# Front of a hybrid decoder block: the row scale of the activations moved to Pool, the first pieces reordered, two streams joined

## The chip, the cores and the metric

The kernel runs on one core of one Trainium2 chip. A core has TensorE (PE: matmul; PEld: its weight loads), VectorE (DVE), ScalarE (ACT), GpSimd (POOL) and SyncE (SP, which here only issues DMAs). The metric is the device time of one execution in microseconds (us).

## The reference

One layer of a decoder block over 256 tokens and 1024 channels, all in float32. `h = rms_norm(x, attn_norm_w)` is projected by one wide matrix `w_in`; slices of the result feed three token mixers: a retention, a gated short convolution and NSA attention (16 heads, 4 key groups). Each mixer's output is projected and gated, the sum goes through an output projection onto `x`, then a convolutional GLU feed-forward block and a last norm follow.

```python
h = rms_norm(x, attn_norm_w)                 # x * rsqrt(mean(x*x) + eps) * w
z = h @ w_in
rq, rk, rv, rg, sb, sc, sx, nq, nkv, ng, mg = split(z)
kc = gelu(blocks(k_c + pos) @ cmp_w1[0]) @ cmp_w2[0]     # compressed keys; vc likewise with index 1
o  = g0 * attend(nq, kc, vc) + g1 * attend_selected(nq, k_s, v_s) + g2 * attend_window(nq, k_w, v_w)
y_sc = sb * causal_dwconv(sc * sx, sc_conv_w)
merged = sigmoid(mg) gates * (y_ret @ w_ret_out, y_sc @ w_sc_out, o @ w_nsa_out)
```

With 4 blocks of 64 tokens and 16 to be selected, every block is selected.

## The kernel before

**Numbers.** Every float32 operand of a matmul is cut into a high and a low part of type fp32r, and a product is three matmuls (`mm3`: high by high, high by low, low by high).

**Pieces.** The weights come in pieces of 1 MB, each two halves of 128x1024 elements. A piece is an `Item`: `load` issues its two DMAs on SP's queue into the ring `raw` of 4 buffers; `split` makes the parts, a cast on ACT (line 131, `whi`) and a subtraction on DVE (line 132, `wlo`), which also frees the raw buffer; `consume` runs the matmuls. Parts lie in a ring of 5 pairs, to which the front adds one more (`w_m`). `stream` walks over a list of items: it loads two ahead, splits one ahead, consumes, and then runs what earlier items put off with `later`. With a generator `gen` it pulls that many steps of the attention after an item as the item's `pull` says.

**Order on the engines.** Within an engine instructions start in queue order. The queues are laid out when the kernel is built, by a planner that has the written order as its priority; so instructions of neighbouring items are interleaved on DVE and ACT, and one that waits holds up those behind it.

**Kinds of piece.** `f_consume` makes 48 matmuls of 128x256 into one PSUM buffer of the ring `mm` (3 buffers), which its `evac` empties. `t_pair` makes two pieces of 24 matmuls of 128x512 each; its first piece takes two buffers of `mm` for both pieces, and the evacuations come with the second. A `w1` piece has 16 matmuls of 128x256 into a buffer of the ring `aux`.

**The front.** The items are, in this order: five pieces `vv` (values and attention gates, on the unscaled `xw`), `kc` and `vc` (also on `xw`; their evacuation multiplies by the row scale `rstd`, line 329, shifts a copy by DMA and makes the blocks `bb` later, lines 346 and 347), `ks` and `kw` (on `hT`, the normed activations), then `g_sc[0]` (a gate of the `mg` columns), `w1` 0, `nq` 0 (queries), `g_sc[1]`, `w1` 1, `g_sc[2]`, `w1` 2, `g_sc[3]`, `w1` 3. `w1` 0 and 1 are the compressed keys' branch and read `bb` of `kc`; `w1` 2 and 3 are the values' and read `bb` of `vc`. The buffers of `mm` go round: `kc`, `vc`, `ks`, `kw` take numbers 0, 1, 2, 0; `g_sc[0]` takes 1 and 2; `nq` 0 takes 0 again.

`head_h` makes `hT` in two halves, ahead of the matmuls of `kc` and of `vc`: for each of 8 blocks of 128 channels DVE multiplies `xT_s` in place by the norm weight `attw(k)` and `rstd` (line 299); for each pair ACT casts to `hTh` (line 302) and DVE subtracts for `hTl` (line 303). `rstd` lies in 128 partitions; it comes from a sum of squares that POOL adds up (lines 270 and 272).

`key_evac` empties `ks` and `kw`: four casts on ACT (line 361, `kdh`) and four subtractions on DVE (line 362, `kdl`) in turn, and four copies to the other half of the partitions, issued on POOL's queue (line 365).

**The attention stream.** After the front its temporary tiles are given back, and a second call of `stream` runs 23 items (`q1 x0 x1 ... n3`: queries, short convolution, its projection, gates) and pulls 36 steps of the attention between them.

Of the kernel before, what the change touches and what calls it, by code (L numbers as in the profile page):

```python
# [13 lines left out]
AF = mybir.ActivationFunctionType  # L14
OP = mybir.AluOpType
# [3 lines left out]
S = 256  # L19
# [44 lines left out]
def kernel(  # L64
# [15 lines left out]
    V, A, T, G = nc.vector, nc.scalar, nc.tensor, nc.gpsimd  # L80

    def f32(ap):
        return ap.bitcast(F32)
# [9 lines left out]
    def bank(tag):  # L93
        t = psum.tile([128, 512], F32, tag=tag, name=f"ps_{tag}", bufs=3 if tag == "mm" else 5)
        return t
# [39 lines left out]
    def halves(name, i):  # L135
        w = wp[_INDEX[(name, i)]]
        return [(w[:, 0:1024], 1024), (w[:, 1024:2048], 1024)]
# [14 lines left out]
    def piece(name, i, consume, **kw):  # L152
        return Item(halves(name, i), consume, **kw)
# [4 lines left out]
    def mm3(o, l, r, start, stop):  # L158
        (lh, ll), (rh, rl) = l, r
        mm(o, lh, rh, start, False)  # L160
        mm(o, lh, rl, False, False)
        mm(o, ll, rh, False, stop)
# [4 lines left out]

        pending.append(f)

    def stream(items, gen=None, la=2, ls=1):  # L170
        n = len(items)
        for i in range(-la, n):
            if 0 <= i + la < n and not items[i + la].raw:
                items[i + la].load()
            if 0 <= i + ls < n and not items[i + ls].parts:
                items[i + ls].split()
            if i < 0:
                continue
            due = pending[:]
            pending.clear()  # L180
            items[i].consume(items[i].parts)
            for f in due:
                f()
            for _ in range(items[i].pull):
                if gen is not None:
                    next(gen, None)

    def f_consume(act, evac, kmajor=False):


        def go(parts):
            ah, al = act() if callable(act) else act
            ps = bank("mm")
            order = [(b, k) for k in range(KB) for b in range(2)] if kmajor else [(b, k) for b in range(2) for k in range(KB)]
            for n, (b, k) in enumerate(order):
                hi, lo = parts[b]
                c = slice(k * 128, (k + 1) * 128)
                o = ps[:, b * 256 : (b + 1) * 256]
                start = n == 0 if kmajor else k == 0
                mm3(o, (hi[:, c], lo[:, c]), (ah[:, k, :], al[:, k, :]), start, k == KB - 1)  # L200
            evac(ps)

        return go
# [28 lines left out]
    hT = [yp.tile([128, KB, S], F32R, tag=n, name=n) for n in ("hTh", "hTl")]  # L232
    M = []
    rstd = yp.tile([128, S], F32, name="rstd")
# [4 lines left out]
    xT_s = x_s[:, HD:].rearrange("p (k t) -> p k t", k=KB)  # L239
# [14 lines left out]
    def attw(k):  # L254
        return attn_w[:, k : k + 1]
# [39 lines left out]
        spread(rs0, sq[:, 1, :], rstd)  # L295

    def head_h(half):
        for k in range(4 * half, 4 * half + 4):
            V.scalar_tensor_tensor(xT_s[:, k, :], xT_s[:, k, :], attw(k), rstd, op0=OP.mult, op1=OP.mult)  # L299
            if k % 2 == 1:  # L300
                c = slice(k - 1, k + 1)
                A.copy(hT[0][:, c, :], xT_s[:, c, :])
                V.tensor_sub(hT[1][:, c, :], xT_s[:, c, :], f32(hT[0][:, c, :]))  # L303


    att_es = ExitStack()
# [43 lines left out]
    def key_evac(name):  # L350
        def evac(ps):
            p4 = ps.rearrange("p (b t) -> p b t", b=2)
            for par in range(2):
                r = slice(par * 64, par * 64 + 64)
                o = slice(64 - par * 64, 128 - par * 64)
                kv4 = [k.rearrange("p (b two) t -> p b two t", two=2) for k in kd]
                for t in range(2):
                    c = KCOL[(name, t)]
                    src = p4[r, :, t * 128 : (t + 1) * 128]
                    dst = [k[r, :, par, c : c + 128] for k in kv4]  # L360
                    A.copy(dst[0], src)
                    V.tensor_sub(dst[1], src, f32(dst[0]))  # L362
                c = min(KCOL[(name, t)] for t in range(2))
                for k in kv4:
                    nc.gpsimd.dma_start(k[o, :, par, c : c + 256], k[r, :, par, c : c + 256])

        return evac
# [3 lines left out]
    def w1_consume(kv, half):  # L371
        def go(parts):
            if half == 0:
                hid[kv] = bank("aux")
            ps = hid[kv][:, 0:256]
            for q, (hi, lo) in enumerate(parts):
                for l in range(4):
                    lp = half * 8 + q * 4 + l
                    c = slice(l * 256, (l + 1) * 256)
                    mm(ps, blk[kv][:, lp, :], hi[:, c], lp == 0, False)  # L380
                    mm(ps, blk[kv][:, lp, :], lo[:, c], False, lp == 15)
            if half == 1:
                compress_act(kv, ps)

        return go
# [253 lines left out]
    def attention():  # L639
        units = []  # L640
        for g in range(4):
            for par in range(2):
                units.append({"g": g, "par": par, "P": {}})
        cur = {}
        for i in range(len(units) + 1):
            u = units[i] if i < len(units) else None
            v = units[i - 1] if i else None
            if u is not None:
                if u["par"] == 0:
                    cur["pc"] = aw.tile([128, 2, 128], F32, tag="pc", name="pc", bufs=2)  # L650
                    V.memset(cur["pc"], 0.0)
                    cur["y"] = aw.tile([128, 2, S], F32, tag="y", name="y", bufs=2)
                u["y"] = cur["y"]
                u["pc"] = cur["pc"]
            for k in range(4):
                if u is not None:
                    soft_step(u, k // 2, k % 2)
                if v is not None:
                    if k < 3:
                        pt_step(v, k)  # L660
                    if k == 0:
                        v["pcT"] = aw.tile([128, S], F32R, tag="ch", name="ch", bufs=2)
                        pc_step(v)
                    if k:
                        av_step(v, k - 1)
                    if k == 3:
                        out_step(v)
                yield
# [38 lines left out]
    def nqp(g, **kw):  # L707
        return piece("nq", g, f_consume(hT, q_evac(g)), **kw)
# [47 lines left out]
    def gate(n, **kw):  # L756

        return [p for c in range(2) for p in t_pair("mg", GATE[n] * 4 + 2 * c, hT, mg_evac(n, c), **kw)]

    def proj(n, **kw):  # L760
        return [p for c in range(2) for p in t_pair(n, 2 * c, lambda: YY[n], o_evac(n, c), **kw)]
# [3 lines left out]
    items = vv + [  # L765
        then(piece("kc", 0, f_consume(xw, cmp_raw_evac(0))), lambda: head_h(0), before=True),
        then(piece("vc", 0, f_consume(xw, cmp_raw_evac(1))), lambda: head_h(1), before=True),
        piece("ks", 0, f_consume(hT, key_evac("ks"))),
        piece("kw", 0, f_consume(hT, key_evac("kw"))),
        g_sc[0],  # L770
        piece("w1", 0, w1_consume(0, 0)),
        nqp(0),
        g_sc[1],
        piece("w1", 1, w1_consume(0, 1)),
        g_sc[2],
        piece("w1", 2, w1_consume(1, 0)),
        g_sc[3],
        piece("w1", 3, w1_consume(1, 1)),
    ]
    then(vv[3], head_rest)  # L780
# [16 lines left out]
    for c in range(4):  # L797
        if c > 1:
            head_chunk(2 * c, 2 * c + 2)
        head_square(c)  # L800
    V.tensor_scalar(rethalf, x_s[:, KB : 2 * KB], 0.5, None, op0=OP.mult)
    stream(items)
    ysc = [yp.tile([128, KB, S], F32R, tag=n, name=n) for n in ("ysch", "yscl")]
    YY.update(o_sc=ysc)
    splitters.pop()
    cp_es.close()
    aw = aw_es.enter_context(pool("aw"))

    att = attention()
    items = []  # L810
    plan = "q1 x0 x1 x4 b0 x2 x3 q2 x6 b1 x5 x7 b2 q3 b3 s0 s1 n0 n1 s2 s3 n2 n3".split()
    p_sc, g_nsa = proj("o_sc"), gate("o_nsa")
    made = {"x": scx, "b": sbp, "q": nqp, "s": lambda j: p_sc[j], "n": lambda j: g_nsa[j]}
    for n, e in enumerate(plan):
        items.append(made[e[0]](int(e[1])))
        items[-1].pull = (36 * (n + 1)) // len(plan) - 36 * n // len(plan)
    stream(items, att)
    for _ in att:
        pass
    assert not pending  # L820
# [121 lines left out]
    items = [piece("r" + n, i, f_consume(hT, rope_evac(n, i))) for n in "qk" for i in range(2)]  # L942
# [20 lines left out]
    x2, hn, ffb = [], [], []  # L963
# [56 lines left out]
    items = []  # L1020
# [117 lines left out]
    for j in range(NF):  # L1138
        act = x2w if j < NX else lambda: h2
        it = piece("up", j, up_early(j) if j < 2 else f_consume(act, up_evac(j)))  # L1140
# [120 lines left out]
```

## Time and profile before

| | |
|---|---|
| Time, median of 3 runs | 633.57 us (632.41 to 634.73) |
| The profiled execution | 633.64 us, of which the profile's span is 631.9 us |
| Busy: PE | 611.0 us (97%) |
| Busy: DVE | 477.9 us (76%) |
| Busy: ACT | 387.9 us (61%) |
| Busy: POOL | 21.2 us (3%) |
| Moved by DMA | 111.80 MB, mean 177 GB/s |

Times in rows count from the start of the span. The profile gives, for an instruction, its start, its duration, and the idle time of its engine just before it with what ended that wait (the last of several). Matmuls are pipelined, so that one's duration is longer than the distance to the next.

### The profile page before, as it was taken

What the parts mean: (1) busy time and instruction counts of PE and PEld (TensorE: products, weight loads), DVE (VectorE), ACT (ScalarE), POOL (GpSimd) and SP (SyncE); (2) the same over time, 40 slices, a digit from 0 to 9 for tenths busy, and PEclk for the clock granted to TensorE, in tenths of its full rate; (3) what the DMA queues carried; (4) which work ended last, traced back from release to release, by engine and by line L of the source; (5) the groups of instructions that cost most, each with busy time, mean ns of one, the idle gap of its engine ahead of it and who ended that gap; (6) DMA issues with size and microseconds to landing.
All of it is one profiled execution on the core that took longest, in us unless ns stands there. A gap on an engine that the chain in (4) does not pass through costs nothing.

```text
span 631.9 us, 10611 instructions
## 1 busy us (share of the span) xinstructions
PE 611.0 (97%) x3948; PEld 554.9 (88%) x3948; DVE 477.9 (76%) x935; ACT 387.9 (61%) x752; POOL 21.2 (3%) x32
## 2 busy tenths in 40 slices
PE   8986999999999999999999999999999999999994
PEld 7986989999999888899888888888999999999993
DVE  5897667898988877679657976568798777777754
ACT  6665666788888887644545565446756555554532
POOL 4202000000000000000000000000000000000001
PEclk8999999999999999999999999999999999999997
DMA  7759876444354344465664477575347655566401
GB/s 247 239 160 271 243 248 206 135 166 135 104 163 135 108 153 140 134 213 169 203 198 160 133 242 260 192 269 172 108 152 264 213 183 175 183 198 199 136 1 66
DMA packets 32995, 111.80 MB, mean 177 GB/s; under 512 B 3632, under 2 KB 5552, under 8 KB 32816
## 3 DMA queue, kind: packets, MB, share of 16 engines
q1 hardware_dynamic: 30240, 106.00, 51.8%
q10 hardware_dynamic: 1552, 4.08, 2.0%
q0 software_dynamic: 1152, 1.05, 1.1%
q8 instruction: 31, 0.51, 0.3%
q14 instruction: 20, 0.16, 0.1%
HBM read 108.50 MB, written 1.05 MB: 173 GB/s over the span
## 4 chain that ended last, share of the span: by engine, by line
PE 82%; DVE 6%; ACT 5%; DMA 4%; POOL 1%; issue 1%; SPq 0%; POOLq 0%; ACTq 0%
PE ps_mm L156 61%; PE ps_aux L156 18%; DMA raw<-in_wp_dram 3%; DVE wlo L132 2%; ACT whi L131 2%; PE ps_aux L589 1%; DMA xT_s<-in_xT_dram 1%; ACT P L566 1%; POOL sq L272 0%; PE ps_aux L618 0%; DVE hTl L303 0%; DVE dd L329 0%; DVE xT_s L299 0%; ACT low L632 0%; DVE bb L347 0%
## 5 line engine op out<-in xcount | busy, mean ns | idle before, releaser
L132 DVE TENSOR_TENSOR wlo<-raw,whi 128x1024 fp32r<-128x1024 f32 (+1 forms) x197 | 237.7, 1210 | 90.7 <-ACT whi L131 88.7
L131 ACT CAST whi<-raw 128x1024 fp32r<-128x1024 f32 (+1 forms) x197 | 203.2, 1035 | 140.0 <-PE ps_mm L156 98.0
L156 PE MATMUL ps_mm<-hTh,whi 128*128 128x256 f32 x352 | 101.0, 287 | 6.1 <-DVE kdl L362 5.1
L156 PE MATMUL ps_mm<-h,whi 128*128 128x256 f32 x576 | 104.0, 283 | 0.0
L156 PE MATMUL ps_mm<-hTl,whi 128*128 128x256 f32 x352 | 100.4, 285 | 0.6 <-DVE hTl L303 0.6
L156 PE MATMUL ps_mm<-hTh,wlo 128*128 128x256 f32 x352 | 100.5, 285 | 0.3 <-DVE wlo L132 0.2
L156 PEld LDWEIGHTS ps_mm<-h,whi 128*128 128x128 f32 x576 | 90.4, 192 | 0.7
L156 PE MATMUL ps_mm<-h,wlo 128*128 128x256 f32 x288 | 81.5, 283 | 0.0
L156 PEld LDWEIGHTS ps_mm<-hTh,whi 128*128 128x128 f32 x352 | 68.1, 193 | 6.7 <-issue 5.2
L156 PEld LDWEIGHTS ps_mm<-hTl,whi 128*128 128x128 f32 x352 | 68.1, 193 | 1.3 <-DVE hTl L303 1.0
L156 PEld LDWEIGHTS ps_mm<-hTh,wlo 128*128 128x128 f32 x352 | 68.1, 194 | 0.7 <-DVE wlo L132 0.7
L156 PE MATMUL ps_mm<-whi,hTh 128*128 128x512 f32 x152 | 59.7, 393 | 0.0
L156 PE MATMUL ps_mm<-wlo,hTh 128*128 128x512 f32 x152 | 59.3, 390 | 0.0
L156 PE MATMUL ps_mm<-whi,hTl 128*128 128x512 f32 x152 | 59.3, 390 | 0.0
L156 PEld LDWEIGHTS ps_mm<-h,wlo 128*128 128x128 f32 x288 | 55.3, 192 | 0.0
L566 ACT ACTIVATE P<-P,st 128x16 f32<-128x16 f32 (+2 forms) x96 | 37.9, 397 | 0.7 <-DVE st L561 0.7
L156 PE MATMUL ps_aux<-wlo,acth 128*128 128x512 f32 x88 | 34.4, 390 | 0.0
L156 PE MATMUL ps_aux<-whi,acth 128*128 128x512 f32 x88 | 34.4, 390 | 0.0
L156 PE MATMUL ps_aux<-whi,actl 128*128 128x512 f32 x88 | 34.3, 389 | 0.0
L156 PEld LDWEIGHTS ps_mm<-whi,hTl 128*128 128x128 f32 x152 | 28.5, 188 | 6.1
L156 PEld LDWEIGHTS ps_mm<-whi,hTh 128*128 128x128 f32 x152 | 28.6, 188 | 5.6
L156 PEld LDWEIGHTS ps_mm<-wlo,hTh 128*128 128x128 f32 x152 | 28.6, 188 | 5.6
(250 smaller groups left out, 1140.9 us busy)
## 6 DMA issues: line engine op xcount, KB each, us to landing
raw<-in_wp_dram SPq DMA_DIRECT2D x194, 512.0 KB, 4.4
raw<-in_wv_dram SPq DMA_DIRECT2D x8, 280.0 KB, 4.8
x2b<-in_xt_dram ACTq DMA_DIRECT2D x1, 1024.0 KB, 7.2
xT_s<-in_xT_dram SPq DMA_DIRECT2D x3, 256.0 KB, 6.9
rct<-in_rc_dram ACTq DMA_DIRECT2D x1, 768.0 KB, 6.1
kdh<-kdh POOLq DMA_DIRECT2D x4, 128.0 KB, 6.1
kdl<-kdl POOLq DMA_DIRECT2D x4, 128.0 KB, 6.9
finb<-in_fin_dram ACTq DMA_DIRECT2D x1, 512.0 KB, 3.5
```

The lines of the kernel that those rows point to most:

```text
L131: A.copy(hi[:, :n], r[:, :n])
L132: V.tensor_sub(lo[:, :n], r[:, :n], f32(hi[:, :n]))
L156: return T.matmul(o, l, r, start=start, stop=stop, skip_group_check=True)
L566: A.activation(pp, pp, AF.Exp, bias=st[:, r : r + 1], scale=-1.0, accum_out=sm[:, r : r + 1])
L589: T.transpose(pt[:, dst : dst + 128], u["P"][(t, pr)][:, c : c + 128], ident)
```

## The change

Three edits, all at the front. In `head_h` the multiplication by `rstd` goes to POOL, for a pair of blocks at a time; the norm weight becomes the scale of the cast on ACT and of the subtraction on DVE, both now for each block. In the list of items `w1` 0 stands directly ahead of the gate pieces, `g_sc[0]` and `g_sc[1]` follow each other, `nq` 0 comes after `w1` 1, and `nq` 1 comes into the front, ahead of `w1` 3, out of the second stream, whose plan has 22 items now. `stream` takes the next stream's first items as `nxt`, and loads and splits them while the front's last items run.

```diff
-    def stream(items, gen=None, la=2, ls=1):
+    def stream(items, gen=None, nxt=(), la=2, ls=1):
         n = len(items)
+        items = items + list(nxt)
         for i in range(-la, n):
-            if 0 <= i + la < n and not items[i + la].raw:
-                items[i + la].load()
-            if 0 <= i + ls < n and not items[i + ls].parts:
+            if 0 <= i + la < len(items):
+                for it in items[max(i, 0) : i + la + 1]:
+                    if not it.raw:
+                        it.load()
+            if 0 <= i + ls < len(items) and not items[i + ls].parts:
                 items[i + ls].split()
...
     def head_h(half):
-        for k in range(4 * half, 4 * half + 4):
-            V.scalar_tensor_tensor(xT_s[:, k, :], xT_s[:, k, :], attw(k), rstd, op0=OP.mult, op1=OP.mult)
-            if k % 2 == 1:
-                c = slice(k - 1, k + 1)
-                A.copy(hT[0][:, c, :], xT_s[:, c, :])
-                V.tensor_sub(hT[1][:, c, :], xT_s[:, c, :], f32(hT[0][:, c, :]))
+        for c in range(2 * half, 2 * half + 2):
+            x2k = xT_s[:, 2 * c : 2 * c + 2, :]
+            G.tensor_tensor(x2k, x2k, rstd.unsqueeze(1).to_broadcast([128, 2, S]), op=OP.mult)
+            for k in (2 * c, 2 * c + 1):
+                A.activation(hT[0][:, k, :], xT_s[:, k, :], AF.Copy, scale=attw(k))
+                V.scalar_tensor_tensor(
+                    hT[1][:, k, :], xT_s[:, k, :], attw(k), f32(hT[0][:, k, :]), op0=OP.mult, op1=OP.subtract
+                )
...
         piece("kw", 0, f_consume(hT, key_evac("kw"))),
+        piece("w1", 0, w1_consume(0, 0)),
         g_sc[0],
-        piece("w1", 0, w1_consume(0, 0)),
-        nqp(0),
         g_sc[1],
         piece("w1", 1, w1_consume(0, 1)),
+        nqp(0),
         g_sc[2],
         piece("w1", 2, w1_consume(1, 0)),
         g_sc[3],
+        nqp(1),
         piece("w1", 3, w1_consume(1, 1)),
...
-    stream(items)
+    att = attention()
+    late = []
+    plan = "x0 x1 x4 b0 x2 x3 q2 x6 b1 x5 x7 b2 q3 b3 s0 s1 n0 n1 s2 s3 n2 n3".split()
...
+    stream(items, nxt=late[:2])
...
-    plan = "q1 x0 x1 x4 b0 x2 x3 q2 x6 b1 x5 x7 b2 q3 b3 s0 s1 n0 n1 s2 s3 n2 n3".split()
...
-    stream(items, att)
+    stream(late, att)
```

## Rows read from the trace of the kernel before

**Rows 1.** The page, busy time and share of each engine.
```profile
PE 611.0 (97%) x3948; PEld 554.9 (88%) x3948; DVE 477.9 (76%) x935; ACT 387.9 (61%) x752; POOL 21.2 (3%) x32
```

**Rows 2.** PE's waits, 0 to 260 us: total, times, longest.
```profile
PE ps_mm L156 <- DVE kdl L362: 5.1, 1, 5.1
```

**Rows 3.** PE's timeline, first matmuls of kc, ks, g_sc[0], nq 0, g_sc[1], w1 1, g_sc[2].
```profile
23.73 0.28 PE L156 MATMUL ps_mm<-ynsah,whi 128*128 128x256 f32 x1
...
35.12 0.28 PE L156 MATMUL ps_mm<-hTh,whi 128*128 128x256 f32 x1
...
49.85 0.40 PE L156 MATMUL ps_mm<-whi,hTh 128*128 128x512 f32 x1
...
62.47 0.55 PE L156 MATMUL ps_mm<-hTh,whi 128*128 128x256 f32 x1 [5.06 <-DVE kdl L362]
...
69.68 0.40 PE L156 MATMUL ps_mm<-whi,hTh 128*128 128x512 f32 x1
...
75.16 0.28 PE L156 MATMUL ps_aux<-whi,bb 128*128 128x256 f32 x1
...
77.08 0.39 PE L156 MATMUL ps_mm<-whi,hTh 128*128 128x512 f32 x1
```

**Rows 4.** Stretches (us): busy (instructions) of each engine, granted PE clock, DMA.
```profile
62.50:69.70 7.20, 7.20 (x49) 7.20 (x50) 3.67 (x3) 2.22 (x3) 0.58 (x1) 0.78 1.12 287
69.70:100.00 30.30, 30.30 (x181) 25.87 (x179) 19.72 (x22) 19.66 (x27) 0.00 (x0) 1.00 0.75 246
...
160.00:240.00 80.00, 78.99 (x544) 72.34 (x543) 68.57 (x221) 67.80 (x191) 0.00 (x0) 1.00 0.41 132
```

**Rows 5.** ACT's timeline behind the kw matmuls.
```profile
59.56 1.04 ACT L131 CAST whi<-raw 128x1024 fp32r<-128x1024 f32 x1 [0.43 <-DMA raw<-in_wp_dram]
60.63 0.37 ACT L361 CAST kdh<-ps_mm 64x256 fp32r<-64x256 f32 x1
```

**Rows 6.** DVE's timeline, 49 to 72 us: subtractions of five halves, last kdl.
```profile
49.88 1.22 DVE L132 TENSOR_TENSOR w_m<-raw,w_m 128x1024 fp32r<-128x1024 f32 x1
...
51.59 1.23 DVE L132 TENSOR_TENSOR wlo<-raw,whi 128x1024 fp32r<-128x1024 f32 x1
...
53.65 1.21 DVE L132 TENSOR_TENSOR wlo<-raw,whi 128x1024 fp32r<-128x1024 f32 x1
...
58.77 1.23 DVE L132 TENSOR_TENSOR wlo<-raw,whi 128x1024 fp32r<-128x1024 f32 x1 [1.22 <-ACT whi L131]
...
61.89 0.43 DVE L362 TENSOR_TENSOR kdl<-ps_mm,kdh 64x256 fp32r<-64x256 f32 x1
...
65.76 1.23 DVE L132 TENSOR_TENSOR wlo<-raw,whi 128x1024 fp32r<-128x1024 f32 x1 [1.88 <-ACT whi L131]
```

**Rows 7.** DVE by line, 22.3 to 45.4 us: busy, mean ns | idle before.
```profile
L299 DVE SCALAR_TENSOR_TENSOR xT_s<-xT_s,rstd 128x256 f32<-128x256 f32 x8 | 3.4, 478 | 0.0
...
L303 DVE TENSOR_TENSOR hTl<-xT_s,hTh 128x512 fp32r<-128x512 f32 x4 | 2.7, 681 | 1.5 <-ACT hTh L302 1.5
...
L470 DVE SCALAR_TENSOR_TENSOR vz<-ps_aux,rs,vz 128x256 fp32r<-128x256 f32 x4 | 1.8, 478 | 0.0
```

**Rows 8.** POOL's timeline, 16 to 20 us.
```profile
17.12 0.74 POOL L270 TENSOR_TENSOR sq<-sq 128x256 f32<-128x256 f32 x1
17.94 1.11 POOL L272 TENSOR_TENSOR sq<-sq 128x256 f32<-128x256 f32 x1
```

**Rows 9.** DVE's timeline, 14 to 23 us.
```profile
15.58 0.73 DVE L132 TENSOR_TENSOR w_m<-raw,w_m 128x560 fp32r<-128x560 f32 x1
...
17.30 2.35 DVE L132 TENSOR_TENSOR wlo<-raw,whi 128x560 fp32r<-128x560 f32 x2
...
21.89 0.42 DVE L286 COPY rstd<-ps_aux 128x256 f32<-128x256 f32 x1 [0.59 <-PE ps_aux L156]
```

**Rows 10.** ACT by line, 22.3 to 45.4 us.
```profile
L131 ACT CAST whi<-raw 128x1024 fp32r<-128x1024 f32 x7 | 7.4, 1051 | 5.0 <-DMA raw<-in_wp_dram 5.0
...
L469 ACT ACTIVATE vz<-ps_aux,rs 128x256 fp32r<-128x256 f32 x4 | 1.7, 473 | 0.0
```

More of the change, by code (lines that the diff above doesn't have):

```diff
@@ L801 @@
     V.tensor_scalar(rethalf, x_s[:, KB : 2 * KB], 0.5, None, op0=OP.mult)
-    stream(items)
+    att = attention()
+    late = []
+    plan = "x0 x1 x4 b0 x2 x3 q2 x6 b1 x5 x7 b2 q3 b3 s0 s1 n0 n1 s2 s3 n2 n3".split()
+    p_sc, g_nsa = proj("o_sc"), gate("o_nsa")
+    made = {"x": scx, "b": sbp, "q": nqp, "s": lambda j: p_sc[j], "n": lambda j: g_nsa[j]}
+    for n, e in enumerate(plan):
+        late.append(made[e[0]](int(e[1])))
+        late[-1].pull = (36 * (n + 1)) // len(plan) - 36 * n // len(plan)
+    stream(items, nxt=late[:2])
     ysc = [yp.tile([128, KB, S], F32R, tag=n, name=n) for n in ("ysch", "yscl")]
@@ L807 @@
     aw = aw_es.enter_context(pool("aw"))
-    att = attention()
-    items = []
-    plan = "q1 x0 x1 x4 b0 x2 x3 q2 x6 b1 x5 x7 b2 q3 b3 s0 s1 n0 n1 s2 s3 n2 n3".split()
[L812 to L816, printed above, removed]
-    stream(items, att)
+    stream(late, att)
     for _ in att:
```

## Prediction

> **What bounds the kernel now.** I read the page first: PE is busy for 97% of the span and the others for 76% or less [rows 1], so an edit pays only where PE stands still or runs slowly. PE's waits say where that is: a single wait of 5.1 us for `kdl`, written at line 362 in the front, is the longest of all [rows 2]. PE's timeline gives the price of a piece there. `kc` and `vc` run from 23.73 to 35.12, 5.70 us each; `g_sc[1]` from 69.68 to 75.16, 5.48; `w1` 1 from 75.16 to 77.08, 1.92 [rows 3]. Against these prices the front loses three times:
>
> - A: `ks` and `kw` take 35.12 to 49.85, 14.73 us for two pieces of 5.70: 3.33 lost [rows 3]. They wait for `hT` and for their own parts.
> - B: 5.06 us of idleness ahead of `nq` 0 at 62.47 [rows 3].
> - C: `nq` 0 takes 62.47 to 69.68, 7.21 us, so 1.51 lost: the granted clock is 0.78 of full speed there, and 1.00 in the stretch after it [rows 4]. 0.78 is a mean over the two levels, 2.4 and 1.2 GHz; the fall came with the idleness of B.
>
> B is no lack of `nq` 0's weights: the subtraction that began at 58.77 made the second half's parts by 60.00. `nq` 0 needs the `mm` buffer that `kw` had, and `kw`'s last `kdl` ran at 61.89 [rows 6]. That one was late since its cast stood on ACT's queue behind the cast of a half for `g_sc[1]`, which waited for its DMA until 59.56 [rows 5]. So B is an evacuation held up by later loads.
>
> **The order of the pieces.** No piece is added: the weights, matmuls and DMAs are the same, and what moves is who stands at which place. After the change `kw` is followed by `w1` 0, `g_sc[0]`, `g_sc[1]`, `w1` 1, and only then `nq` 0 asks for `kw`'s buffer: 1.92 + 5.48 + 5.48 + 1.92 = 14.8 us after `kw`, where it was 7.4. Behind 49.85 that is 64.65, later than the `kdl` that ended at 62.32. So B goes, and C with it, since no long idleness is left: 6.57 us.
>
> What is late next is the weights, as the pieces that PE eats fast come earlier. I keep the times at which DVE frees halves before (the places in the load order stay; other pieces stand in them) and walk PE along them, from 49.85:
>
> - `w1` 0, in the first place: its second half is ready at 51.10 (49.88 + 1.22), needed at 50.81. Wait 0.29; end 52.06.
> - `g_sc[0]`, second place: 51.59 + 1.23 = 52.82, wait 0.76. Its second half is needed a quarter of a piece later, at 54.19, and comes at 53.65 + 1.21 = 54.86, wait 0.67; end 58.97.
> - `g_sc[1]`, third: its second half comes at 60.00, needed at 60.34. No wait; end 64.45.
> - `w1` 1 starts at once and ends at 66.37.
> - `nq` 0, fifth: its first half comes at 65.76 + 1.23 = 66.99, wait 0.62 [rows 6].
>
> From there no place is late against PE, which in the order before never stands still from 69.70 to 100 [rows 4]. New waits: 0.29 + 0.76 + 0.67 + 0.62 = 2.34. Net gain of the order: 6.57 - 2.34 = 4.2 us. `w1` 0 reads the blocks `bb` of `kc`; they come out of DVE ahead of `kw`'s parts, and `kw` itself runs between, so I cost that need at nothing; if they came late, `w1` 0 would stand still by just that.
>
> **The row scale.** DVE loses eight products of line 299, 3.4 us, and four subtractions of line 303, 2.7 us; it gets eight `scalar_tensor_tensor` of 128x256, priced as line 299's, 3.4 us. Net -2.7. DVE also sat for 1.5 us ahead of line 303, waiting for ACT's cast [rows 7]; with the product done early that wait can go: at best -4.2.
>
> Against this stands POOL's product on 128x512, four times. The trace has no such instruction. The nearest are sums of 128x256, of 0.74 and 1.11 us [rows 8]. With twice the elements I take twice the time, 1.5 to 2.2 us each and 5.9 to 8.9 for four; from `rstd`, written at 22.31 [rows 9], that reaches to 28.2 or 31.2, ahead of `ks` at 35.12 either way. POOL has nothing else then; its next work, the copies of `ks`, comes after `ks`.
>
> But POOL's sums slow DVE. Two subtractions of 128x560 took 2.35 us beside two POOL sums, and one alone takes 0.73 [rows 8, 9]: 0.89 us lost while POOL ran for 1.67 us of them (17.30 to 17.86 and 17.94 to 19.05), so 0.53 a microsecond. For 5.9 us of products that is 3.1 us. So DVE comes out at -4.2 + 3.1 = -1.1 us. The bounds: -4.2 if nothing is lost, and if all 5.9 us are lost and the 1.5 us wait stays, -2.7 + 5.9 = +3.2.
>
> The Trainium skill (SBUF — State Buffer, section "SBUF: two separate sides") says that a DVE instruction with two SBUF inputs and a POOL instruction that reads SBUF take a shared pair of ports in turns, one blocked fully while the other runs. The row's 0.53 lies below that. By the rule the four products would cost DVE their full 5.9 us but for what fits beside instructions with one SBUF tensor, and the sum would be about 1 us better than before instead of 5; that is the second rival.
>
> DVE's parts set both when `ks` and `kw` run (A) and when raw buffers come free (the places above). So what DVE gains is worth itself, up to A's 3.33; -1.1 gives 1.0 us, a little rounded down as PE's 2.34 of new waits depend on loads too.
>
> **At nothing.** ACT gets eight scaled casts, at 0.47 us from line 469 3.8 us in all, in place of four; even all of it fits in the 5.0 us that ACT waits for raw halves in this stretch [rows 10]. Without that cover it is 3.8 us at most, less the four casts. The joined streams: the seam before lies within 69.70 to 100, where PE is busy 30.30 of 30.30 us [rows 4], so there is nothing to gain; SP issues the same loads in a row, and `x0` and `x1` only come earlier in the written order. `nq` 1 keeps its length. The attention's 36 steps lie between 22 items instead of 23, 4.5% denser; DVE is busy 68.57 of 80 us there and PE 78.99 [rows 4], so up to 1 us could be lost; I take none and put it in the range.
>
> **Sum.** The profiled execution took 633.64 us, of which 631.9 are the span, and it lies 0.07 from the median, 633.57. 633.64 - 4.2 - 1.0 = 628.4.
>
> **Rivals.**
>
> - *All of the relief pays.* POOL's products run beside DVE's instructions that read PSUM, such as line 470 with 1.8 us [rows 7], and cost little. DVE is 4.2 us earlier, A's 3.33 go, the gain is 7.5: 626.1. If also the loads come earlier by that, all of A, B and C go, 9.9: 623.7. For it: A is long and DVE's. Against: [rows 9].
> - *POOL takes the time that it gives.* DVE is 3.2 us later, `kw` and the places shift by that: 4.2 - 3.2 = 1.0, 632.6. The skill's rule leads here. For it: DVE's work in this stretch is mostly subtractions of two tensors in SBUF.
> - *DVE stands in its queue* (slower). If the planner puts the eight `hTl` ahead of the parts of `vc`, DVE waits for POOL's last product, and `vc` with all loads behind it comes late. With a product of P us POOL ends at 22.3 + 4P and the first part of `vc` is there 1.2 us later; PE wants it at 23.73 + 5.70 = 29.43. The delay is 4P - 5.9, and everything behind shifts by it. It eats the order's 4.2 from P = 2.5 on; P = 3.0 gives 6.1 and 635.5, from where the kernel is measurably slower; P = 3.2 gives 636.3. For it: nothing passes in a queue, and [rows 5] show an evacuation caught that way. Against: 2.2 is the most that [rows 8] give.
>
> **Numbers.** The forecast has 0.52, the full relief 0.18, POOL taking its time 0.18, the slower queue 0.12. 0.3%, 1.9 us, is about what a measurement of this kernel can tell from no change; so faster is below 631.7, slower above 635.5. The first two cases are faster; of the third 0.05 lies below 631.7 and 0.13 within; of the fourth 0.03 is within. Faster 0.75, same 0.16, slower 0.09. The range takes in the full relief with the loads, 623.7, and most of the third case: 624 to 633.5. The forecast's own is 626 to 630.5.
>
> **What would show it.** In the profile after: no wait for `kdl` above 1 us ahead of a piece on `mm`, and no granted clock below 1.00 between 20 and 100 us; waits of 0.3 to 0.8 us for parts ahead of `g_sc[0]` and `nq` 0; POOL's products of 1.5 to 2.2 us, done by 31; DVE's `wlo` of `ks` and `kw` at about the times before, less 1. It would be wrong if `kw` ends later than 49.85, if ACT's queue holds `kw`'s evacuation past 64, or if waits of over 2 us turn up ahead of the gates.

## The result, and the profile after

| | before | after |
|---|---|---|
| Median (lowest to highest) of 11 runs each | 633.78 us (631.84 to 636.56) | 629.65 us (627.65 to 631.55) |
| Profiled execution, span | 633.64 us, 631.9 us | 631.34 us, 629.6 us |

The ratio is 0.9937, with an interval of 0.992 to 0.9953: the change is faster by 4.1 us. The forecast was 628.4 us, and the time lies in its own range. The profiled execution of after is 1.69 us above the median of its runs, so its trace shows a poor sample of the changed kernel; the profiled pair differs by 2.3 us only.

PE's waits of after from 20 to 100 us (in total, times, longest) are what answers to [rows 2]:

```profile
PE ps_mm L156 <- DVE wlo L132: 3.7, 4, 1.6
PE ps_aux L156 <- ACT cq_lo L412: 1.2, 1, 1.2
PE ps_aux L156 <- DVE w_m L132: 0.9, 1, 0.9
PE ps_aux L434 <- DVE cq_lo L425: 0.8, 1, 0.8
PE ps_aux L156 <- DVE sq L288: 0.3, 1, 0.3
```

The wait for `kdl` is gone, and many short ones stand in its place. PE's timeline tells where they are: the first matmuls of `kc`, `ks`, `w1` 0, then a matmul in `g_sc[0]`, the first of `w1` 1's second half, one of `nq` 0, two of the compressed keys' small products, and the first of `x0`.

```profile
22.86 0.29 PE L156 MATMUL ps_mm<-ynsah,whi 128*128 128x256 f32 x1
...
34.38 0.28 PE L156 MATMUL ps_mm<-hTh,whi 128*128 128x256 f32 x1
...
48.26 0.28 PE L156 MATMUL ps_aux<-whi,bb 128*128 128x256 f32 x1
...
53.95 0.50 PE L156 MATMUL ps_mm<-wlo,hTh 128*128 128x512 f32 x1 [1.61 <-DVE wlo L132]
...
65.68 0.50 PE L156 MATMUL ps_aux<-w_m,bb 128*128 128x256 f32 x2 [0.88 <-DVE w_m L132]
...
67.61 0.39 PE L156 MATMUL ps_mm<-hTh,wlo 128*128 128x256 f32 x1 [0.60 <-DVE wlo L132]
...
74.57 0.65 PE L156 MATMUL ps_aux<-cq_lo,cmt 128*64 128x256 f32 x2 [1.18 <-ACT cq_lo L412]
...
83.61 0.33 PE L434 MATMUL ps_aux<-ident,cq_lo 64*128 64x64 f32 x2 [0.79 <-DVE cq_lo L425]
...
97.56 0.27 PE L156 MATMUL ps_mm<-hTh,whi 128*128 128x256 f32 x1
```

`ks` and `kw` take 34.38 to 48.26, 13.88 us, where they took 14.73 [rows 3]: 0.85 gained. The new waits behind `kw` are 1.61 + 0.88 + 0.60 + 1.18 + 0.79 = 5.06 us, where 2.34 were forecast: by chance the very size of the wait that went away. The stretches of after, with the columns of [rows 4], show what was won all the same:

```profile
62.50:69.70 7.20, 5.73 (x41) 5.12 (x40) 4.08 (x4) 4.72 (x6) 1.16 (x2) 1.00 0.97 241
69.70:100.00 30.30, 28.33 (x188) 25.52 (x188) 21.37 (x24) 19.94 (x28) 0.00 (x0) 1.00 0.79 261
160.00:240.00 80.00, 79.16 (x535) 72.18 (x534) 68.24 (x222) 67.55 (x195) 0.00 (x0) 1.00 0.41 136
28.00:45.00 17.00, 15.47 (x124) 14.90 (x123) 16.88 (x25) 12.51 (x17) 1.49 (x1) 1.00 0.60 179
45.00:57.00 12.00, 10.38 (x65) 8.85 (x64) 8.44 (x11) 4.61 (x8) 2.53 (x4) 1.00 1.08 247
57.00:70.00 13.00, 11.53 (x67) 9.74 (x67) 7.31 (x8) 7.75 (x10) 2.32 (x4) 1.00 1.01 244
```

The granted clock is 1.00 where it was 0.78, and with it the 1.51 us of loss C are gone; the stretch from 69.70 on, which had no idleness, now has 1.97 us. For this pair 6.57 removed, less 5.06, plus 0.85 from `ks` and `kw`, is 2.4 beside the 2.3 of the two times; but that agreement is luck. After's profiled execution is already 0.87 us ahead where `kc` starts (22.86, 23.73 before [rows 3]), before anything that was changed, and the sum leaves that out. With it some 0.9 us of loss is missing; most of it lies in `g_sc[0]` and `g_sc[1]`, which take 50.18 to 63.57, 13.39 us, where two prices of 5.48 and the wait of 1.61 make 12.57. That part of PE's time shows as no wait. In the attention (160 to 240 us) PE is busy as before.

The row scale is seen on POOL's timeline, with the four products in one row, and below it the third and the fourth by themselves:

```profile
21.53 7.97 POOL L304 TENSOR_TENSOR xT_s<-xT_s,rstd 128x512 f32<-128x512 f32 x4 [1.69 <-DVE rstd L290]
...
25.93 1.31 POOL L304 TENSOR_TENSOR xT_s<-xT_s,rstd 128x512 f32<-128x512 f32 x1
...
27.21 2.28 POOL L304 TENSOR_TENSOR xT_s<-xT_s,rstd 128x512 f32<-128x512 f32 x1
```

and DVE's timeline beside them:

```profile
22.83 1.98 DVE L132 TENSOR_TENSOR wlo<-raw,whi 128x1024 fp32r<-128x1024 f32 x1 [0.25 <-ACT whi L131]
24.74 1.26 DVE L476 SCALAR_TENSOR_TENSOR vz<-ps_aux,rs,vz 128x256 fp32r<-128x256 f32 x3
25.91 0.17 DVE L503 TENSOR_SCALAR sg<-sg 128x48 f32<-128x48 f32 x1
26.01 2.32 DVE L132 TENSOR_TENSOR wlo<-raw,whi 128x1024 fp32r<-128x1024 f32 x1
28.25 1.28 DVE L503 TENSOR_SCALAR sg<-sg 128x48 f32<-128x48 f32 x1
```

A product takes 1.99 us in the mean, and the last ends at 29.50. Two subtractions take 1.98 and 2.32 us where one takes 1.22, and a small multiplication 1.28 where its like takes 0.17: 0.76 + 1.10 + 1.11 = 2.97 us lost, and 3.1 were forecast. POOL loses as well. The third product, which began with no subtraction running, took 1.31 us; the fourth began inside the subtraction of 26.01 to 28.33 and took 2.28, and that subtraction had begun inside the third product and ended 1.09 us after it. So the two take turns, and 1.99 is a mean with POOL's waiting in it.

### The profile page after: what moved, and what is told of

Same layout as the page of the kernel before. It is cut to its first block, busy times and chain, and to the rows that moved or that the text cites. A ratio compares the mean times of both kernels' runs of the same rounds, so it can differ in the third digit from the quotient of the medians.

```text
span 629.6 us, 10620 instructions
## 1 busy us (share of the span) xinstructions
PE 609.4 (97%) x3948; PEld 552.5 (88%) x3948; DVE 477.7 (76%) x931; ACT 388.3 (62%) x756; POOL 29.2 (5%) x36
## 4 chain that ended last, share of the span: by engine, by line
PE 81%; DMA 6%; DVE 5%; ACT 4%; issue 1%; POOL 0%; SPq 0%; POOLq 0%; ACTq 0%
PE ps_mm L156 61%; PE ps_aux L156 17%; DMA raw<-in_wp_dram 5%; DVE wlo L132 2%; PE ps_aux L595 2%; ACT whi L131 2%; DMA xT_s<-in_xT_dram 1%; ACT P L572 1%; DVE w_m L132 0%; DVE hTl L307 0%; DVE dd L335 0%; ACT ynsah L266 0%; ACT w_m L131 0%; PE ps_aux L624 0%; DVE hnb L1002 0%
## 5 line engine op out<-in xcount | busy, mean ns | idle before, releaser
L156 PE MATMUL ps_mm<-wlo,hTh 128*128 128x512 f32 x160 | 62.7, 392 | 1.6 <-DVE wlo L132 1.6
L156 PE MATMUL ps_mm<-whi,hTh 128*128 128x512 f32 x160 | 63.2, 395 | 0.0
L156 PE MATMUL ps_mm<-whi,hTl 128*128 128x512 f32 x160 | 62.5, 390 | 0.0
L156 PEld LDWEIGHTS ps_mm<-wlo,hTh 128*128 128x128 f32 x160 | 30.1, 188 | 8.3 <-DVE wlo L132 2.2
L156 PEld LDWEIGHTS ps_mm<-whi,hTh 128*128 128x128 f32 x160 | 30.1, 188 | 6.8 <-ACT whi L131 0.5
L156 PEld LDWEIGHTS ps_mm<-whi,hTl 128*128 128x128 f32 x160 | 30.0, 188 | 6.3
```

The costliest lines, as they stand in the source:

```text
L156: return T.matmul(o, l, r, start=start, stop=stop, skip_group_check=True)
```

## The experiments

Twelve runs. Each ratio is to the kernel before as measured beside it (medians 633.46, 633.27 and 633.57 us in the groups e1, e2 and e3), with its interval; ratios are compared below, not medians of different groups. PE's busy time is that from 20 to 100 us of the profiled execution, and so are the clock (mean granted) and the longest wait of PE. One profiled execution can lie 2 us off the median, that of e3_raw6_before even 5.9, so its own time stands there too.

| run | median us | ratio | profiled us | PE busy of 80 | clock | longest wait |
|---|---|---|---|---|---|---|
| before | 633.78 | 1 | 633.64 | 72.72 | 0.98 | 5.1 `kdl` |
| after | 629.65 | 0.9937 (0.992 to 0.9953) | 631.34 | 73.11 | 1.00 | 1.6 `wlo` |
| e1_order_only | 629.26 | 0.9942 (0.991 to 0.9973) | 629.26 | 76.21 | 0.98 | 1.0 `hTh` |
| e1_pool_only | 631.75 | 0.9967 (0.9951 to 0.9983) | 633.27 | 72.22 | 0.98 | 4.5 `kdl` |
| e1_join_only | 633.21 | 0.9987 (0.997 to 1.0003) | 634.61 | 71.20 | 0.96 | 6.9 `kdl` |
| e1_no_pool | 631.09 | 0.9954 (0.9935 to 0.9972) | 628.89 | 75.55 | 1.00 | 1.4 `cq_lo` |
| e2_kw_bank | 632.76 | 0.9985 (0.9967 to 1.0003) | 630.52 | 75.08 | 0.98 | 2.4 `thg` |
| e2_nq_late | 632.40 | 0.9981 (0.9964 to 0.9999) | 631.54 | 74.68 | 0.98 | 2.1 `cq_lo` |
| e2_late_kd | 631.80 | 0.9972 (0.9956 to 0.9988) | 631.52 | 74.48 | 0.98 | 3.1 `cq_lo` |
| e2_late_kd_before | 634.04 | 1.0013 (0.9995 to 1.0032) | 635.47 | 74.52 | 0.94 | 3.1 `kdl` |
| e3_nq_w1 | 632.70 | 0.9981 (0.9964 to 0.9998) | 633.04 | 74.52 | 0.96 | 2.8 `cq_lo` |
| e3_raw6_before | 628.39 | 0.9922 (0.9896 to 0.9948) | 634.29 | 73.55 | 0.94 | 2.2 `whi` |
| e3_raw6 | 625.37 | 0.9875 (0.9861 to 0.989) | 624.83 | 78.27 | 1.00 | 0.9 `wlo` |
| e3_raw6_late_kd | 626.29 | 0.9892 (0.9877 to 0.9906) | 626.14 | 78.07 | 1.00 | 0.9 `wlo` |

### Which of the three edits pays

**e1_order_only**: the kernel before with the new list of pieces and the shorter plan, and neither POOL's products nor the join.

```diff
-        g_sc[0],
         piece("w1", 0, w1_consume(0, 0)),
-        nqp(0),
+        g_sc[0],
         g_sc[1],
         piece("w1", 1, w1_consume(0, 1)),
+        nqp(0),
...
+        nqp(1),
...
-    plan = "q1 x0 x1 x4 b0 x2 x3 q2 x6 b1 x5 x7 b2 q3 b3 s0 s1 n0 n1 s2 s3 n2 n3".split()
+    plan = "x0 x1 x4 b0 x2 x3 q2 x6 b1 x5 x7 b2 q3 b3 s0 s1 n0 n1 s2 s3 n2 n3".split()
```

> The kernel before with the second edit alone: the front's items in the new order (w1 0 ahead of the gates, nq 0 after w1 1, nq 1 in the front), row scale on DVE, streams not joined. If the order carries the gain (the prediction's step: 6.57 us of B and C go, 2.34 us of new waits come), it is about 4 us faster than before, ratio 0.993 to 0.995, and the wait for kdl ahead of nq 0 is gone. If the row scale on POOL carried it, this is within 0.3% of before.

**e1_pool_only**: the kernel before with the new `head_h` alone.

```diff
-            V.scalar_tensor_tensor(xT_s[:, k, :], xT_s[:, k, :], attw(k), rstd, op0=OP.mult, op1=OP.mult)
...
+            G.tensor_tensor(x2k, x2k, rstd.unsqueeze(1).to_broadcast([128, 2, S]), op=OP.mult)
...
```

> The kernel before with the first edit alone: the row scale on POOL. If the port is worth about 1 us to DVE (prediction), within 0.3% of before, ratio 0.997 to 1.000, with the wait for kdl of about 5 us still there. If the relief of DVE carries the gain: 0.990 to 0.994. If POOL takes more than it gives: 1.001 to 1.005.

**e1_join_only**: the kernel before with the joined streams alone (`nq` 1 stays the first of the second stream).

```diff
-    stream(items)
...
+    stream(items, nxt=late[:2])
...
```

> The kernel before with the third edit alone: the front's last items load and split the first two items of the attention stream. Prediction: nothing, ratio 0.998 to 1.002, since PE does not stand still at the seam. If the seam hid a wait: below 0.997.

**e1_no_pool**: the changed kernel with the old `head_h`, the row scale on DVE.

```diff
-            G.tensor_tensor(x2k, x2k, rstd.unsqueeze(1).to_broadcast([128, 2, S]), op=OP.mult)
...
+            V.scalar_tensor_tensor(xT_s[:, k, :], xT_s[:, k, :], attw(k), rstd, op0=OP.mult, op1=OP.mult)
...
```

> The changed kernel with the row scale back on DVE: order and joined streams alone. If POOL's part is worth 1 us, it is 0.1 to 0.2% slower than the changed kernel, ratio to before about 0.995. If POOL's products cost DVE what they relieve, it equals the changed kernel, 0.993 to 0.994; if they cost more, it is faster, 0.990 to 0.993.

The order alone gives 3.7 us (0.0058 of 633.78), where 4.2 were forecast. Its profiled execution is its median, and PE's waits there from 20 to 100 us are a better sample of the new order than after's own:

```profile
PE ps_mm L156 <- ACT hTh L302: 1.0, 1, 1.0
PE ps_mm L156 <- DVE wlo L132: 0.7, 2, 0.3
PE ps_aux L156 <- ACT cq_lo L406: 0.7, 1, 0.7
PE ps_aux L428 <- DVE cq_lo L419: 0.6, 1, 0.6
PE ps_mm L156 <- DVE hTl L303: 0.6, 2, 0.3
PE ps_aux L156 <- DVE sq L284: 0.3, 1, 0.3
```

The waits for `hTh` and `hTl` are part of A and stand so in the trace of before too; here the granted clock falls behind them, to 0.50 from 40 to 42 us, and `ks` and `kw` take 15.63 us. New are 0.7 + 0.7 + 0.6 = 2.0 us, near the 2.34 of the forecast, but only 0.7 of them are for weights. The scale on POOL alone gives 2.1 us, twice what it was priced at, with a wait for `kdl` of 4.5 us left; on top of the order and the join it gives 1.1 (0.9937 against 0.9954), and those two intervals overlap. The join alone can't be told from nothing.

### Is it the buffer of `kw`

**e2_kw_bank**: the order of before, but `kw` accumulates in a buffer of `aux`, so that `nq` 0 needs none of `kw`'s.

```diff
-            ps = bank("mm")
+            ps = bank(tag)
...
-        piece("kw", 0, f_consume(hT, key_evac("kw"))),
+        piece("kw", 0, f_consume(hT, key_evac("kw"), tag="aux")),
```

> The kernel before, with nothing but kw's PSUM buffer taken from the ring aux instead of mm, so that nq 0 no longer asks for kw's buffer. If B is kw's evacuation held up behind casts (my theory), the wait for kdl goes without any change of order: nq 0 starts at about 57.6 to 58 us, as its parts come, and 5 to 6.5 us are saved, ratio 0.990 to 0.992. If B is a lack of weights that kdl only masks, the wait is renamed to parts and the ratio stays at 0.998 or above.

**e2_nq_late**: the order of before, only `nq` 0 behind `w1` 1.

```diff
-        nqp(0),
         g_sc[1],
         piece("w1", 1, w1_consume(0, 1)),
+        nqp(0),
```

> The kernel before with one move of the second edit: nq 0 behind w1 1; w1 0 stays behind the first gate piece and nq 1 in the second stream. If the move of nq 0 away from kw's evacuation is what the order brings, this gives about all of the order's gain, ratio 0.993 to 0.996. If w1 0 ahead of the gates matters, less than half: above 0.997.

**e3_nq_w1**: the same, and `w1` 0 ahead of `g_sc[0]`; so the new order without `nq` 1 in the front.

```diff
-        g_sc[0],
         piece("w1", 0, w1_consume(0, 0)),
-        nqp(0),
+        g_sc[0],
         g_sc[1],
         piece("w1", 1, w1_consume(0, 1)),
+        nqp(0),
```

> The kernel before with nq 0 behind w1 1 and w1 0 ahead of the first gate piece; nq 1 stays in the second stream. Against the move of nq 0 alone (0.998) and the whole order (0.994): if w1 0's place is what makes the difference, 0.993 to 0.996; if it is nq 1 in the front, 0.997 to 0.999.

In e2_kw_bank the place of the wait is just as the prediction had it: PE's timeline has `nq` 0 directly behind `w1` 0, at 54.91 and so sooner than expected.

```profile
54.79 0.29 PE L156 MATMUL ps_aux<-wlo,bb 128*128 128x256 f32 x1
54.91 0.27 PE L156 MATMUL ps_mm<-hTh,whi 128*128 128x256 f32 x1
```

The 5.1 us are gone, and yet the ratio is 0.9985, with 1 in its interval, where 0.990 to 0.992 were expected. Nor was the wait renamed to parts, as in the other case expected. PE's waits, 0 to 260 us, say what came instead:

```profile
PE ps_mm L156 <- ACT thg L719: 2.4, 1, 2.4
PE ps_aux L428 <- DVE cq_lo L419: 1.5, 2, 1.2
```

`thg` empties the buffers of the first two gate pieces, and `g_sc[2]` needs one of them. ACT's timeline:

```profile
67.51 1.05 ACT L131 CAST whi<-raw 128x1024 fp32r<-128x1024 f32 x1 [1.91 <-DMA raw<-in_wp_dram]
68.82 1.04 ACT L131 CAST whi<-raw 128x1024 fp32r<-128x1024 f32 x1 [0.26 <-DMA raw<-in_wp_dram]
69.89 0.59 ACT L523 ACTIVATE qs<-ps_mm 64x512 fp32r<-64x512 f32 x1
70.39 0.58 ACT L719 ACTIVATE thg<-ps_mm 128x512 f32<-128x512 f32 x1
```

That is [rows 5] over again with another evacuation: two casts wait for their loads, 1.91 and 0.26 us, and what frees PSUM stands behind them. The granted clock from 70 to 80 us is 0.83, so C came back as well. e2_nq_late and e3_nq_w1 show the pattern at `cq_lo` of the compressed keys' branch, with 2.1 and 2.8 us. In these three runs removing B is worth 0.15 to 0.19%, barely more than nothing, and the place of `w1` 0 makes no difference (0.9981 twice). So B was the place where PE met the late loads, and not the cause of the loss.

### What makes the loads late

Two candidates: the copies that `ks` and `kw` issue on POOL's queue, which run beside the loads of the gates, and the raw buffers, which DVE gives back late.

**e2_late_kd**: the changed kernel, with those copies held until a small POOL product that reads a result of the compressed keys' branch, behind `w1` 1. **e2_late_kd_before**: the same in the kernel before.

```diff
-                    nc.gpsimd.dma_start(k[o, :, par, c : c + 256], k[r, :, par, c : c + 256])
+                    copies.append((k[o, :, par, c : c + 256], k[r, :, par, c : c + 256]))
...
+            first = G.tensor_tensor(gate2, zr[:, 0:2], mhalf, op=OP.mult)
+            with tc.issue_after(first.ins):
+                for o, i in copies:
+                    nc.gpsimd.dma_start(o, i)
```

> The changed kernel with the eight copies of ks and kw held on POOL's queue until w1 1 has been evacuated (behind a small POOL instruction that reads its copy), instead of between the raw loads. In the changed kernel raw halves land in 7.6 to 9.3 us while the copies run and 4 to 5 us else. If the copies slow the loads, halves land in some 5 us up to w1 1, the waits for parts ahead of g_sc[0], w1 1 and nq 0 (1.6, 0.9, 0.6) shrink to under 0.5 each, and it is 2 to 4 us faster than the changed kernel, ratio to before 0.987 to 0.991. If the loads are at the limit of HBM anyway, no change: 0.993 to 0.995. If the copies now hold up the attention's first step, slower than that.

> The kernel before with the copies held the same way. If they are the cause of the late loads that kw's evacuation stands behind, B shrinks from 5.1 to about 2 to 3 us and the ratio is 0.993 to 0.997. If B does not hang on the copies: 0.998 to 1.002, with the wait for kdl unchanged.

DMA issues of after from 48 to 68 us (count, size, median us from issue to landing):

```profile
raw<-in_wp_dram SPq DMA_DIRECT2D x8, 512.0 KB, 8.1
kdl<-kdl POOLq DMA_DIRECT2D x4, 128.0 KB, 7.4
...
```

and of e2_late_kd, first from 48 to 68 us, then from 72 to 86 us, where the copies now run:

```profile
raw<-in_wp_dram SPq DMA_DIRECT2D x11, 512.0 KB, 5.5
...
raw<-in_wp_dram SPq DMA_DIRECT2D x5, 512.0 KB, 9.3
kdl<-kdl POOLq DMA_DIRECT2D x4, 128.0 KB, 13.5
...
```

Beside the copies a load takes longer, by 2.6 us in this pair. The size varies from execution to execution: with the copies in place the median of the same stretch is 6.6 in before and only 5.6 in e1_no_pool and e3_nq_w1, and without them it is 5.4 in e2_late_kd_before. Without them the waits behind `kw` up to `w1` 1 nearly vanish (PE is busy 11.35 of 12.00 us from 45 to 57, and 12.86 of 13.00 up to 70). But the collision moves. ACT's timeline of e2_late_kd, where the copies are:

```profile
81.67 1.05 ACT L131 CAST whi<-raw 128x1024 fp32r<-128x1024 f32 x1 [3.60 <-DMA raw<-in_wp_dram]
83.68 1.05 ACT L131 CAST whi<-raw 128x1024 fp32r<-128x1024 f32 x1 [0.96 <-DMA raw<-in_wp_dram]
85.95 1.04 ACT L131 CAST w_m<-raw 128x1024 fp32r<-128x1024 f32 x1 [1.22 <-DMA raw<-in_wp_dram]
87.02 0.28 ACT L442 ACTIVATE cq_lo<-ps_aux 128x128 f32<-128x128 f32 x1
```

PE waits 3.1 us for that last one, and the granted clock from 85 to 92 us is 0.79. In the changed kernel the delay costs 2.2 us (0.9972 against 0.9937, intervals apart). In e2_late_kd_before B shrinks only to 3.1 us, with no copy beside the loads, and the ratio is 1.0013, where 0.993 to 0.997 were expected of copies that cause B. So the copies are not the main cause.

**e3_raw6**: the changed kernel, with two more raw buffers. They lie in a tile that is free between the sum of squares and the second stream; four pieces use them in turn (`ks`, `g_sc[0]`, `nq` 0, `g_sc[3]`). **e3_raw6_before**: the same in the kernel before (`ks`, `w1` 0, `w1` 1, `g_sc[3]`). **e3_raw6_late_kd**: e3_raw6 with the delayed copies.

```diff
+            if self.extra:
+                two = yp.tile([128, 2, 1024], F32, tag="yscl", name="raw_x")
...
+    for j in (7, 10, 13, 16):
+        items[j].extra = True
```

> The changed kernel with two more raw buffers in the front, in the room of the sums of squares: every third piece from ks on (ks, g_sc[0], nq 0, g_sc[3]) is loaded there. If the new waits come from loads that are issued late, since DVE frees the four buffers late between 28 and 49 us while DMA is not full, loads up to nq 0 are issued 4 to 7 us earlier, the waits for parts (1.6, 0.9, 0.6) and for the compressed branch behind casts (1.2, 0.8) go to under 0.5 each, and it is 2 to 4 us faster than the changed kernel: ratio to before 0.987 to 0.991. If the memory's rate is the limit, no change: 0.993 to 0.995.

> The kernel before with the same two more raw buffers. If B is kw's evacuation behind casts that wait for loads, earlier loads let the evacuation pass and B shrinks to under 2 us: ratio 0.991 to 0.995. If B is in the order of ACT's queue whatever the loads do, the wait for kdl stays at 4 us or more and the ratio is above 0.998.

> Both: two more raw buffers in the changed kernel, and the copies of ks and kw held until w1 1 is evacuated. Holding the copies alone moved the waits behind w1 1, where the copies then met the loads (0.997). If the buffers let PE's parts be made ahead of that meeting, 0.986 to 0.991; if the copies cost the same wherever they meet the loads, above 0.993.

e3_raw6 is the best of all, 625.37 us in the median of four runs, and beats both kernels by more than the intervals. PE's waits from 20 to 100 us are these and no others:

```profile
PE ps_mm L158 <- DVE wlo L134: 1.5, 2, 0.9
PE ps_aux L158 <- DVE sq L290: 0.3, 1, 0.3
PE ps_aux L436 <- DVE cq_lo L427: 0.2, 1, 0.2
```

The 1.5 us lie within `ks` and `kw`; behind them 0.2 us of waiting is left, where after has 5.06. The stretches answer to the last three of after:

```profile
28.00:45.00 17.00, 15.48 (x124) 14.92 (x123) 16.85 (x25) 12.84 (x18) 1.00 (x1) 1.00 0.68 202
45.00:57.00 12.00, 11.94 (x72) 10.29 (x71) 9.94 (x13) 7.13 (x11) 3.09 (x5) 1.00 1.09 260
57.00:70.00 13.00, 13.00 (x88) 11.69 (x87) 8.84 (x9) 7.52 (x10) 1.75 (x4) 1.00 1.19 285
```

From 28 to 45 us DVE is full in both (16.88 and 16.85 of 17.00 us). With four buffers that means that loads are not issued: the DMA share is 0.60 in after and 0.68 here. The halves of `g_sc[0]` are issued at 36.0 and 36.4 us here, and at 42.7 and 43.8 in after, as SP's queue shows, here and then in after:

```profile
36.02 0.80 SPq L126 DMA_DIRECT2D raw_x<-in_wp_dram  x2
...
42.66 1.46 SPq L124 DMA_DIRECT2D raw<-in_wp_dram  x2
```

A half still takes long beside the copies (median 9.3 us for those in the ring, 48 to 68 us), but it was asked for in time; and as more is moved (260 and 285 GB/s, 247 and 244 in after), the memory's rate was not the limit. The kernel before gains from the buffers too: 4.9 us (0.9922), where the three edits bring 4.1; the intervals overlap. Its profiled execution is the slowest of its nine, with halves landing in a median of 11.5 us and a wait of 2.2 us for `whi`, so its trace is no fair sample. With the buffers the three edits still count (0.9922 without, 0.9875 with them, intervals apart), and holding the copies back gains nothing (0.9892 against 0.9875).

## Why the prediction was right, and where its working was not

- **B and C** went as said, with `kdl`'s wait and the clock of 0.78, and three signs held: no clock below 1.00 in after, `kw` ended at 48.26, no wait above 2 us. The wait in `g_sc[0]` was 1.61 us, where 0.3 to 0.8 were expected. e2_kw_bank shows that the reason was the right one: with another buffer for `kw`, and nothing else changed, `nq` 0 doesn't wait. It also shows that 6.57 us is not what B and C are worth wherever they are removed: there it was 1.0, as the late loads met PE elsewhere.
- **The price of the order** was right as a net (3.7 alone, 4.2 forecast). Its term of new waits, 2.34 us, is the one that was mis-sized: 5.06 in after's profiled execution, 2.0 in that of e1_order_only. The second is near it by luck, as 1.3 of its 2.0 us are for `cq_lo`, which the forecast did not have. The step that failed is "From there no place is late against PE". In each of the three traces with the new order, four raw buffers and the copies in place (after, e1_order_only, e1_no_pool) the compressed branch waits for `cq_lo`, a copy on ACT and then the last step of a gelu on DVE, which stand behind the weights' casts and subtractions: 1.18 + 0.79, 0.7 + 0.6 and 0.5 + 1.4 us. I had walked PE along the weights only, and not along the evacuations; and I kept the places at the times of before, though the halves behind `kw` landed in 8.1 us in after and in 6.6 in before.
- **The row scale**: POOL's products were priced at 1.5 to 2.2 us and take 1.99, but by luck: alone a product took 1.31 us, less than that, and the rest is waiting for DVE, which the sum did not have. DVE's loss was priced at 3.1 and is 2.97; A's gain at 1.0, and `ks` with `kw` gained 0.85. All five traces with the scale on POOL have 13.85 to 13.88 us for `ks` and `kw`. Those with it on DVE have 14.24 to 14.73 us in four, 15.63 to 16.01 in the three where the granted clock fell there (e1_order_only, e3_nq_w1, e2_late_kd_before), and 13.62 and 13.68 in e3_raw6_before and e2_kw_bank. As a whole 1.1 us remain on top of the order, within its uncertainty.
- **What I priced at nothing**: the join (0.9987, the interval holds 1), `w1` 0's need for `bb`, ACT's eight scaled casts, and the denser attention (PE 79.16 of 80 us busy, 78.99 before [rows 4]) cost nothing that is seen.
- **The rivals.** Full relief would have taken all of A, and `ks` with `kw` keep 2.48 of its 3.33 us; with the loads it would have left no waits, and the trace has 5.06 us of them. That POOL takes what it gives is refuted by e1_pool_only, which is faster. DVE did not stand in its queue for POOL: line 307 follows the weights' part at 31.12 without idleness.

The row on POOL also bears on the rule cited ahead. The Trainium skill (SBUF — State Buffer, section "SBUF: two separate sides") has whichever of the two starts first hold the shared ports for its whole instruction while the other waits, if DVE's has two inputs in SBUF, or is in a two-port mode, and POOL's reads SBUF. The trace fits that both ways: the multiplication that began at 28.25 ends at 29.53, right behind POOL's last product (29.50), and that product had itself waited for a subtraction, while line 476, which reads PSUM, keeps 0.42 us each. The prediction set its 0.53 against the rule, but [rows 8, 9] show turns as well: POOL's second sum, begun inside a subtraction, took 1.11 us where another took 0.74. DVE lost 2.97 us and not all of the 7.97, as POOL's time holds its own waiting and DVE had line 476 to do.

**Settled**: loads that come late because raw buffers are given back late are what holds this front back: two more buffers leave 0.2 us of waiting behind `kw` in the changed kernel, and make either kernel faster. **Open**: why the whole new order (0.9942) does better than the parts of it in e2_nq_late and e3_nq_w1 (0.9981 each). The difference left to e3_nq_w1 is `nq` 1 in the front; the intervals overlap. In the profiled executions those two have waits above 2 us and a clock below 1.00, and after has neither, so that short and scattered waits may be cheaper than one long one with a fall of the clock; but e1_order_only has a fall too (0.98), behind its wait of 1.0 us for `hTh`. One execution of each does not settle it.

## What to carry to other kernels

A long wait for an evacuation names where PE met the shortage, and not what is short: look at what the evacuating engine itself stood behind, and if that is a load, at when the load was issued and which buffer it had waited for. Where a reordering removes one wait, walk PE along everything that it needs at the new places, the small copies of side branches as well as the weights. Where DVE is full and the DMA share is low, look for room for one more pair of buffers: here it was worth 3.9 us on top of the three edits and 4.9 without them, about what the new order brought (3.7) or more.

## What the runs showed of the hardware that I had not expected

- A small DVE instruction with one tensor in SBUF (128x48) took 1.28 us when it began inside POOL's product, and 0.17 when it began 0.02 us ahead of one: it isn't only the long subtractions that stand still.
- POOL's products lose to DVE's subtractions too: 1.31 us alone, 2.28 when one began inside a subtraction.
- Loads of 512 KB landed in a median of 5.4 and 5.5 us with no copies on POOL's queue beside them (48 to 68 us), and in 5.6 to 11.5 with them, though these are only 128 KB each; and the copies themselves took 7.2 to 7.4 us at one place and 13.5 to 13.9 where they were issued in a row.
